# Kept slots leave the ring of weight buffers, and the output projection's last column block of the second token tile runs in two halves

## The chip, the core and the metric

The kernel runs on one core of a Trainium2 chip. Its time is the device time of one execution in microseconds (us), and the figure that counts is the median of several runs. The core has five engines that run side by side and wait for one another through semaphores. PE (TensorE) multiplies matrices. DVE (VectorE), ACT (ScalarE) and POOL (GpSimd) work element by element. SP (SyncE) issues nearly all of the DMA transfers, one after the other: a transfer that has to wait holds up every transfer behind it.

## What is computed

The input is 256 tokens of 2048 numbers, all float32. One block is computed: an RMS norm, an input projection, two kinds of attention heads, an output projection that is added to the input, and then a mixture of 32 experts in four groups. A router picks the best group and in it the best two experts for each token. What matters here is cut from the reference:

```python
x = x + mixed @ w_out[layer]
h = rms_norm(x, ffn_norm_gain[layer])
x = x + hierarchical_moe(h, w_group_router[layer], b_group_router[layer], ...)
...
g_prob = softmax(t @ w_group_router + b_group_router)        # 4 groups, top 1
e_all  = t @ w_expert_router + b_expert_router               # 32 experts, top 2 in the group
hid = jax.nn.silu(t @ wg) * (t @ wu)                         # for each of 32 experts
acc = acc + c[:, None] * (hid @ wd)
...
return rms_norm(x, final_norm_gain)
```

Every expert's three weight matrices (2048x512, 2048x512 and 512x2048, 4 MB each) are read from memory once, 384 MB in all.

## The kernel before, in words

The tokens lie in two tiles of 128, in `x2[:, t]`. The program has three stages: the input projection and the attention (up to about 280 us), the output projection with norm and router, and the experts (from about 415 us).

**Output projection, norm and router.** `w_out` is taken in four row quarters and in each in four column blocks of 512 (NB = 4). Only the last quarter matters here. `unit_parts` (L233) loads a piece of weights and splits it into a high and a low part (`wh`, `wl`), and `rows3` (L273, products in L277 to L279) multiplies high by high, low by high and high by low into one accumulator `acc` per token tile. After a column block, DVE adds the accumulator to `x2`. Between these products PE does the router's work on the blocks that are ready: `norm_T` (L578) squares the block on ACT for the norm's sum (`ss2`), transposes it on PE (L584) and copies it out on ACT (`hrT`, L586), and `logits` (L589, L593) multiplies it by the router's weights into `lg`. The last column block (L609 to L625) runs all its products for token tile 0, adds them (L622), runs all for tile 1, adds them, and then does `norm_T` and `logits` for both tiles. Nine products without use (L630) keep PE busy afterwards. DVE waits for `lg` and for the reciprocal root that POOL takes (`rst`, L156), and runs a chain of some twenty short operations (L646 to L732) up to the matrix `S0`, which gathers the tokens of the first two experts.

**Experts.** The loop at the end of the program takes two experts at a time, 16 pairs e = 0, 2, ..., 30. A pair runs its gate products (`pg`, 64 matmuls), its up products (`pu`, 64), gathers the next pair's tokens, and runs its down products (`y`, 64); a pair's results are added to `x2` while the next pair runs (`scatter`, L863; `yh` and `yl` are the weighted results, L859 and L860). Nearly all matmuls of this stage are issued by the helper `mm` (L761), in the order in which the program writes them (`keep_in_program_order`); the tile names tell them apart. The other engines' order, and SP's, comes from a scheduler.

**The ring.** The weights of a pair come in 12 loads of 2 MB, each into a slot of 16 KB per partition from `next_slot` (L748). The first 12 slots come from the list `first` (L744). After that the list `order`, which is `first` without `ring_h` and `ring_e`, is gone round: two slots from the pool `ring_r`, one from `ring_c`, four from `ring_a`, one from `ring_c`, two from `ring_d`. That is ten entries for ten buffers. A load into a buffer waits until PE has used what lay there.

Two of the slots are not for weights. In pair e = 28, `gates` takes one (L982) for the final gain and the output rows of token tile 0 (`gfin`, `fo[0]`). It is slot 172 of the count (14 pairs of 12, and 4 loads), which is the first entry of the list, `ring_r`, and it is kept to the program's end. In the last pair `down_cols` takes slot 193 for the output rows of token tile 1 (`fo[1]`, L1048). The list goes on as if both were ordinary: slots 182 and 183, the second and third gate load of the last pair, are `ring_r` again, slot 192 (the last down columns) is `ring_r`, and so is slot 193. With the kept slot in it, `ring_r` has one buffer left, which all four of these use.

**The end.** The last pair's down products run by columns (`down_cols`, L1023): four cuts of 512, 512, 512 and 384 columns and one of 128 (j = 0 to 4). `finish(j)` adds cut j to `x2` and calls `final_block` (L918): ACT squares the cut for the final norm and writes the squares into `fo[t]` (L921), then DVE (t = 0) or POOL (t = 1) overwrites that with the row times the gain (L924). `final_store` (L926) takes the reciprocal root, scales the rows and stores them.

Of the kernel before, what the change touches and what calls it, by code (L numbers as in the profile page):

```python
# [13 lines left out]
F32 = mybir.dt.float32  # L14
# [3 lines left out]
AF = mybir.ActivationFunctionType  # L18
OP = mybir.AluOpType
# [3 lines left out]
P = 128  # L23
T = 256
D = 2048
KC = D // P
NB = 4
# [53 lines left out]
def block_kernel(ctx: ExitStack, tc: tile.TileContext, a: dict, out: bass.AP):  # L81
    nc = tc.nc
    sync, act, dve, pe, pool = nc.sync, nc.scalar, nc.vector, nc.tensor, nc.gpsimd
    scale = 1.0 / math.sqrt(HD)

    con = ctx.enter_context(tc.tile_pool(name="con", bufs=1))
    ring_a = ctx.enter_context(tc.tile_pool(name="ring_a", bufs=NA))

    def slot(pl):
        return pl.tile([P, 4096], F32, tag="slot", name="slot")  # L90
# [27 lines left out]
    x2 = con.tile([P, 2, D], F32, name="x2")  # L118
# [154 lines left out]
    def rows3(accs, lh, ll, wh, wl, start, stop, tiles=(0, 1)):  # L273

        for t in tiles:
            tt = slice(t * P, (t + 1) * P)
            pe.matmul(accs[t], lh[:, tt], wh, start=start, stop=False)  # L277
            pe.matmul(accs[t], lh[:, tt], wl, start=False, stop=False)
            pe.matmul(accs[t], ll[:, tt], wh, start=False, stop=stop)  # L279
# [287 lines left out]
    sync.dma_start(wr, a["w_router"])  # L567
    sync.dma_start(c4, a["consts4"])
    dve.tensor_tensor(wr, wr, gfn[:, :, None].to_broadcast([P, KC, NG + NE]), op=OP.mult)
    ss2 = con.tile([P, 2, NB], F32, name="ss2")  # L570
    lg = rt_ps.tile([P, 2, NG + NE], F32, name="lg")

    def pt2():
# [1 line left out]

    hTs = {}

    def norm_T(b, t):  # L578

        sq = rt.tile([P, 512], BF, name="sq2")  # L580
        act.activation(sq, x2[:, t, b * 512:(b + 1) * 512], AF.Square, accum_out=ss2[:, t, b:b + 1])
        pt = pt2()
        for i in range(4):
            pe.transpose(pt[:, i * P:(i + 1) * P], x2[:, t, b * 512 + i * P:b * 512 + (i + 1) * P], ident)  # L584
        hT = rt.tile([P, 4, P], F32, name="hrT", bufs=2)
        act.activation(hT.rearrange("p a b -> p (a b)"), pt, AF.Copy)  # L586
        hTs[b, t] = hT

    def logits(b, t):  # L589
        for i in range(4):  # L590
            c = 4 * b + i

            pe.matmul(lg[:, t], hTs[b, t][:, i], wr[:, c], start=c == 0 and t == 0, stop=c == KC - 1 and t == 1,  # L593
                      skip_group_check=True)

    def tick0(b):
# [11 lines left out]

    accs = acc2()  # L609
    parts = list(unit_parts(a["w_out"], 3, (NB - 1) * 512))  # L610
    for t in range(2):
        for hf, wh, wl in parts:
            for j in range(2):
                c = 2 * hf + j
                rows3(accs, mh[3][:, c], ml[3][:, c], wh[:, j], wl[:, j], c == 0, c == 3, (t,))
            if t == 0:
                (tick0, tick1)[hf](NB - 1)
            elif hf == 0:
                logits(NB - 2, 0)
                logits(NB - 2, 1)  # L620
        xb = x2[:, t, (NB - 1) * 512:]
        dve.tensor_tensor(xb, xb, accs[t], op=OP.add)  # L622
    norm_T(NB - 1, 0)
    norm_T(NB - 1, 1)
    logits(NB - 1, 0)  # L625
    logits(NB - 1, 1)

    wps = pt2()
    for _ in range(NKEEP):
        pe.matmul(wps[:, :T], ident, hTs[NB - 1, 1][:, :2], start=True, stop=True)  # L630


    rst = con.tile([P, 2], F32, name="rst")
# [108 lines left out]
    y_ps = ctx.enter_context(tc.tile_pool(name="y_ps", bufs=4, space=PSUM, reuse_waits="tile"))  # L742

    first = [ring_r, ring_r, ring_c, ring_a, ring_h, ring_a, ring_e, ring_a, ring_a, ring_c, ring_d, ring_d]  # L744
    order = [q for q in first if q not in (ring_h, ring_e)]
    units = [0]

    def next_slot():  # L748
        units[0] += 1
        u = units[0] - 1  # L750
        return slot(first[u] if u < len(first) else order[(u - len(first)) % len(order)])

    def ps_m():
        return m_ps.tile([P, 512], F32, tag="m", name="m")
# [215 lines left out]
    def gates(e, gather_first):  # L970

        last = e == NE - 2
        pg = gu_ps.tile([P, F], F32, name="pg")
        pu = gu_ps.tile([P, F], F32, name="pu")
        for b in range(4):
            if gather_first is not None:
                hT[b] = gather(gather_first, b, 2 if e == 0 else 1)
            gate_up(pg, a["w_gate"], e, b)
        scatter_done((0, 1))
        cT = scatter_mat(sels_of(e))  # L980
        if e == NE - 4:
            z = next_slot()  # L982
            gfin[0], fo[0] = z[:, :D], z[:, D:]
            for b in range(NB):
                final_gain(b)
        for b in range(4):
            gate_up(pu, a["w_up"], e, b, last and b > 1)
            if last and b < 2:
                scatter_done((b + 2,))
        if e == 0:  # L990
            keep_rows()
        return cT, hidden(pg, pu, 2 if last else 1)
# [30 lines left out]
    def down_cols(e, cT, hid):  # L1023


        cuts = [(0, 512), (512, 1024), (1024, 1536), (1536, 1920), (1920, D)]
        w = {}
        for h in range(2):
            z = next_slot().rearrange("p (e c n) -> p e c n", e=2, c=2)
            for i in range(2):  # L1030
                sync.dma_start(z[:, i], a["w_down"][e + i, h * 256:h * 256 + 256, :1024]
                               .rearrange("(c p) n -> p c n", p=P))
                for j in range(2):
                    for c in range(2):
                        w[j, i, 2 * h + c] = z[:, i, c, j * 512:j * 512 + 512]
        for j in range(2, 5):
            n0, n1 = cuts[j]
            n = n1 - n0
            if n0 % 512 == 0:
                z = next_slot()  # L1040
                at0 = 0
            for i in range(2):
                zi = z[:, at0:at0 + 4 * n].rearrange("p (c n) -> p c n", c=4)
                at0 += 4 * n
                sync.dma_start(zi, a["w_down"][e + i, :, n0:n1].rearrange("(c p) n -> p c n", p=P))
                for c in range(4):
                    w[j, i, c] = zi[:, c]
        fo[1] = next_slot()[:, :D]  # L1048
        py = [ps_y() for _ in cuts[:4]]

        def products(j, cs):
            n = cuts[j][1] - cuts[j][0]
            for c in cs:
                for i in range(2):
                    mm(py[j][C * i:C * i + C, :n], hid[:, c, C * i:C * i + C], w[j, i, c],
                       start=c == 0, stop=c == 3)

        def finish(j):
            n0, n1 = cuts[j]

            scatter(cT, weighted(cT, py[j], n1 - n0), n0, n1,
                    lambda t: gu_ps.tile([P, F], F32, name="pu" if j % 2 else "pg") if t else ps_m())
            final_block(n0, n1, j)

        for h in range(2):
            for j in range(2):
                products(j, (2 * h, 2 * h + 1))
        for j in range(2, 5):
            if j == 4:
                py.append(ps_y())  # L1070
            finish(j - 2)
            products(j, range(4))
        finish(3)
        finish(4)
        final_store(len(cuts))
# [106 lines left out]
```

## Time and profile before

| | |
|---|---|
| median of 3 runs | 1364.29 us (1363.77 to 1365.88) |
| profiled execution, its own time | 1366.4 us |
| its span on the core | 1364.6 us |
| mean granted clock of PE | 0.988 of full speed |
| PE busy | 1308.2 us (96%) |
| ACT, DVE, POOL busy | 274.0, 491.8, 13.6 us |
| moved by DMA | 478.42 MB, mean 351 GB/s |

The profile is of one execution. Its page gives a string of digits for each engine: the span in 40 slices of 34.1 us, and in each the busy share in tenths. A busy PE is not a PE at its peak, since matmuls overlap and their ends are modelled. The views that answer questions about a place are the timeline (instructions by start time, what the engine waited for in brackets) and the stretches (busy time, clock and DMA rate between two times).

### The profile page before, as it was taken

Reading aid. Unit: us, or ns where it says so; the run is one execution under the profiler, and the core shown is the slowest. Engines: PE = TensorE matmul, PEld = TensorE weight load, DVE = VectorE, ACT = ScalarE, POOL = GpSimd, SP = SyncE. Lnnn points to the kernel's source line nnn. Section 1 sums busy time; section 2 is a strip of 40 time slices with the busy share of each in tenths; the row PEclk is TensorE's granted clock in tenths of the full one; section 3 lists DMA queues with packets and bytes.
Section 4 is the critical chain, followed back from the end, with each engine's and each line's share of the span. In section 5 each row is a group of like instructions: output and inputs, shape, how many; then the busy total and the mean of one; then the engine's idle time right before and its main releaser. Section 6 shows DMA issues by size and latency. Waiting matters only on the chain. (4 is left out here: it accounts for less than half of the span.)

```text
span 1364.6 us, 16713 instructions
## 1 busy us (share of the span) xinstructions
PE 1308.2 (96%) x7155; PEld 768.1 (56%) x7155; DVE 491.8 (36%) x906; ACT 274.0 (20%) x454; POOL 13.6 (1%) x22
## 2 busy tenths in 40 slices
PE   9999999999999999999999999999999999999885
PEld 8999998988885444535535444343543434343432
DVE  5555567677643121222322213212221322122123
ACT  6454445354340100000000000000000000001002
POOL 0000000000000000000000000000000000000001
PEclk9999999999999999999999999999999999998988
DMA  9973554446969799999999999999999999999793
GB/s 357 332 261 127 182 186 148 161 166 237 324 232 392 296 428 426 426 427 427 426 427 427 426 426 427 425 427 427 426 428 426 426 428 426 425 427 427 293 407 107
DMA packets 77223, 478.42 MB, mean 351 GB/s; under 512 B 5204, under 2 KB 8148, under 8 KB 53336
## 3 DMA queue, kind: packets, MB, share of 16 engines
q1 hardware_dynamic: 76848, 476.73, 86.0%
q8 instruction: 58, 0.95, 0.3%
q10 hardware_dynamic: 296, 0.56, 0.1%
q14 instruction: 21, 0.17, 0.0%
HBM read 475.18 MB, written 2.10 MB: 350 GB/s over the span
## 5 line engine op out<-in xcount | busy, mean ns | idle before, releaser
L761 PE MATMUL pu<-slot,hT 128*64 128x512 f32 x1024 | 235.2, 601 | 13.5 <-DMA slot<-in_w_up 13.5
L761 PE MATMUL pg<-slot,hT 128*64 128x512 f32 x1024 | 234.3, 598 | 12.3 <-DMA slot<-in_w_gate 12.3
L761 PE MATMUL y<-slot,hid 128*64 128x512 f32 (+2 forms) x1040 | 223.9, 587 | 0.1
L761 PEld LDWEIGHTS pg<-slot,hT 128*64 128x64 f32 x1024 | 75.3, 138 | 165.7 <-issue 153.5
L870 DVE TENSOR_TENSOR x<-x,y 128x512 f32<-128x512 f32 x120 | 75.9, 684 | 252.4 <-PE y L761 252.4
L761 PEld LDWEIGHTS pu<-slot,hT 128*64 128x64 f32 x1024 | 73.9, 138 | 163.7 <-issue 142.8
L761 PEld LDWEIGHTS y<-slot,hid 128*64 128x64 f32 x1040 | 72.8, 137 | 138.5 <-issue 136.0
L257 DVE TENSOR_TENSOR wl<-slot,wh 128x1024 fp32r<-128x1024 f32 (+1 forms) x100 | 117.6, 1181 | 81.5 <-ACT wh L256 81.0
L294 PE MATMUL acc<-xh,wh 128*128 128x256 f32 x512 | 131.5, 289 | 0.0
L294 PE MATMUL acc<-xl,wh 128*128 128x256 f32 x512 | 128.2, 283 | 0.0
L256 ACT ACTIVATE wh<-slot 128x1024 fp32r<-128x1024 f32 (+1 forms) x100 | 101.9, 1025 | 124.5 <-PE acc L279 72.6
L761 PE MATMUL m<-S,slot 128*128 128x128 f32 x960 | 113.7, 277 | 4.7 <-DVE hT L805 4.7
L761 PEld LDWEIGHTS m<-S,slot 128*128 128x128 f32 x960 | 110.5, 192 | 9.7 <-DVE hT L805 7.6
L860 DVE SCALAR_TENSOR_TENSOR yl<-y,ws,yh 128x512 fp32r<-128x512 f32 (+1 forms) x65 | 46.9, 741 | 166.7 <-ACT yh L859 165.1
L294 PEld LDWEIGHTS acc<-xl,wh 128*128 128x128 f32 x512 | 98.0, 191 | 0.4
L294 PEld LDWEIGHTS acc<-xh,wh 128*128 128x128 f32 x512 | 97.9, 191 | 0.5
L859 ACT ACTIVATE yh<-y,ws 128x512 fp32r<-128x512 f32 (+1 forms) x65 | 44.2, 680 | 254.9 <-PE y L761 254.9
L294 PE MATMUL acc<-xh,wl 128*128 128x256 f32 x512 | 82.3, 283 | 0.0
L838 DVE TENSOR_TENSOR sg<-sg,pu 128x512 f32<-128x512 f32 (+1 forms) x17 | 11.1, 655 | 192.6 <-PE pu L761 184.3
L805 DVE TENSOR_TENSOR hT<-m,smallp 128x512 f32<-128x512 f32 (+1 forms) x68 | 44.9, 660 | 91.7 <-PE m L761 91.7
L851 ACT ACTIVATE hid<-m 128x512 f32<-128x512 f32 (+1 forms) x17 | 9.7, 572 | 323.5 <-PE m L764 323.5
L294 PEld LDWEIGHTS acc<-xh,wl 128*128 128x128 f32 x512 | 70.6, 192 | 0.0
(215 smaller groups left out, 1131.8 us busy)
## 6 DMA issues: line engine op xcount, KB each, us to landing
slot<-in_w_down SPq DMA_DIRECT2D x60, 2048.0 KB, 32.6
slot<-in_w_gate SPq DMA_DIRECT2D x60, 2048.0 KB, 36.8
slot<-in_w_up SPq DMA_DIRECT2D x58, 2048.0 KB, 30.6
slot<-in_w_in SPq DMA_DIRECT2D x46, 1024.0 KB, 7.3
slot<-in_w_out SPq DMA_DIRECT2D x16, 1024.0 KB, 5.3
slot<-in_w_up SPq DMA_DIRECT2D x10, 1024.0 KB, 11.6
slot<-in_w_gate SPq DMA_DIRECT2D x8, 1024.0 KB, 9.6
slot<-in_w_down SPq DMA_DIRECT2D x6, 1024.0 KB, 16.1
```

Of the source, the lines that this page charges most:

```text
L256: act.activation(wh[:, k:k + n], src[:, k:k + n], AF.Copy)
L257: dve.tensor_sub(wl[:, k:k + n], src[:, k:k + n], wh[:, k:k + n].bitcast(F32))
L294: pe.matmul(o, wz[:, i * P:(i + 1) * P], x, start=k == 0 and i % 2 == 0 and wz is wh and x is h, stop=k == KC - 1 and i % 2 == 1 and wz is ...
L761: tc.keep_in_program_order(pe.matmul(*args, **flags))
L805: dve.tensor_tensor(hT[:, j * n:(j + 1) * n], p.rearrange("p (a b) -> p a b", a=n), (gfp if hp_ else gfn)[:, c:c + n, None].to_broadcast([ ...
L838: dve.tensor_tensor(sg[:, q], sg[:, q], pu[:, q], op=OP.mult)
L851: act.activation(hid[:, j * n:(j + 1) * n].rearrange("p c q -> p (c q)"), p[:, :n * P], AF.Copy)
L859: act.activation(yh[:, :n], py[:, :n], AF.Copy, scale=ws)
L860: dve.scalar_tensor_tensor(yl[:, :n], py[:, :n], ws, yh[:, :n].bitcast(F32), op0=OP.mult, op1=OP.subtract)
L870: dve.tensor_tensor(xb, xb, p[:, :n], op=OP.add)
```

## The change

`next_slot` now takes entries off the front of a queue and puts them back at its end, unless the slot is kept (or is `ring_h` or `ring_e`). The slots for `gfin` and `fo[0]`, and for `fo[1]`, are asked for with `keep=True`. After slot 172 the queue therefore holds nine entries: one `ring_r` and the eight others.

The output projection's last column block is written out anew. Token tile 0 runs as before. Token tile 1 runs in two halves of 256 columns: twelve products for a half, an addition of 256 columns to `x2`, then norm, transposes and the copy of that half. `norm_T` and `logits` take the range of 128-column pieces to work on, and `ss2` has a fifth column for the second half's sum, and is zeroed once by POOL.

```diff
-    ss2 = con.tile([P, 2, NB], F32, name="ss2")
+    ss2 = con.tile([P, 2, NB + 1], F32, name="ss2")
+    pool.memset(ss2, 0.0)
...
-    def norm_T(b, t):
+    def norm_T(b, t, i0=0, i1=4):
...
-    for t in range(2):
+    for hf, wh, wl in parts:
+        for j in range(2):
+            c = 2 * hf + j
+            rows3(accs, mh[3][:, c], ml[3][:, c], wh[:, j], wl[:, j], c == 0, c == 3, (0,))
+        (tick0, tick1)[hf](last)
+    xb = x2[:, 0, last * 512:]
+    dve.tensor_tensor(xb, xb, accs[0], op=OP.add)
+
+    for s in range(2):
+        n0 = s * 256
         for hf, wh, wl in parts:
             for j in range(2):
                 c = 2 * hf + j
...
+                o, h, l = accs[1][:, n0:n0 + 256], mh[3][:, c, P:], ml[3][:, c, P:]
+                for k, (x, w) in enumerate(((h, wh), (h, wl), (l, wh))):
+                    pe.matmul(o, x, w[:, j, n0:n0 + 256], start=s == 0 and c == 0 and k == 0,
+                              stop=s == 1 and c == 3 and k == 2, skip_group_check=True)
+            if hf == 0:
+                logits(last - 1, s)
+        xb = x2[:, 1, last * 512 + n0:last * 512 + n0 + 256]
+        dve.tensor_tensor(xb, xb, accs[1][:, n0:n0 + 256], op=OP.add)
+        if s == 0:
+            norm_T(last, 0)
+            norm_T(last, 1, 0, 2)
+        else:
+            logits(last, 0)
+            end = norm_T(last, 1, 2, 4)
+    logits(last, 1)
...
-    def next_slot():
-        units[0] += 1
-        u = units[0] - 1
-        return slot(first[u] if u < len(first) else order[(u - len(first)) % len(order)])
+    ring = deque(first)
+
+    def next_slot(keep=False):
+
+        q = ring.popleft()
+        if not keep and q not in (ring_h, ring_e):
+            ring.append(q)
+        return slot(q)
...
-            z = next_slot()
+            z = next_slot(keep=True)
...
-        fo[1] = next_slot()[:, :D]
+        fo[1] = next_slot(keep=True)[:, :D]
```

SP's queue, kernel before, at the loads of the last pair. A slot's number names the load, `DMAHW` is a transfer that must have landed and `PE_49` a matmul that must be done. `slot_7665` and `slot_7683` are the second and third gate load:

```order
L895 DMA slot_7665<-in_w_gate 128x4096 [waits DMAHW5_49,DMAHW4_49,PE_49]
L895 DMA slot_7685<-in_w_gate 128x4096 [waits PE_49]
L895 DMA slot_7735<-in_w_up 128x4096 [waits DMAHW6_49,PE_49]
L895 DMA slot_7683<-in_w_gate 128x4096 [waits DMAHW7_49,DMAHW4_49,PE_49]
L895 DMA slot_7737<-in_w_up 128x4096 [waits DMAHW0_49]
L887 DMA slot_7775<-in_w_up 128x2048 [waits DMAHW1_49]
```

The same place in the changed kernel, where the gate loads are `slot_7682` to `slot_7704`:

```order
L913 DMA slot_7684<-in_w_gate 128x4096 [waits DMAHW5_49,DMAHW4_49,PE_49]
L913 DMA slot_7702<-in_w_gate 128x4096 [waits PE_49]
L913 DMA slot_7704<-in_w_gate 128x4096 [waits DMAHW6_49,PE_49]
L913 DMA slot_7754<-in_w_up 128x4096 [waits DMAHW7_49,PE_49]
L913 DMA slot_7756<-in_w_up 128x4096 [waits DMAHW0_49,PE_49]
L905 DMA slot_7794<-in_w_up 128x2048 [waits DMAHW1_49,PE_49]
```

The third gate load stood behind the first up load and waited for the matmuls of the second gate load, whose buffer it takes; the loads behind it waited for no matmul. Now the four gate loads stand together, and each load behind them waits for the matmuls of the load that had its buffer nine entries earlier.

PE's queue at the end of the output projection, kernel before (L277 to L279 the products of token tile 1, L584 transposes, L593 router products, L630 the products without use):

```order
L277 MATMUL acc<-wh,mh 128x512
L278 MATMUL acc<-wl,mh 128x512
L279 MATMUL acc<-wh,ml 128x512
L584 MATMUL pt<-c_78,x_80 128x128 x8
L593 MATMUL lg<-wr,hrT 128x36 x8
L630 MATMUL pt<-hrT,c_78 128x256 x9
```

The same place in the changed kernel (L631 the products of half a block, L586 transposes, L597 router products):

```order
L631 MATMUL acc<-wh,mh 128x256
L631 MATMUL acc<-wl,mh 128x256
L631 MATMUL acc<-wh,ml 128x256
L597 MATMUL lg<-wr,hrT 128x36 x6
L586 MATMUL pt<-c_78,x_80 128x128 x2
L597 MATMUL lg<-wr,hrT 128x36 x2
L647 MATMUL pt<-hrT,c_78 128x256 x9
```

Of the last block's eight transposes, six have moved ahead of the second half's products, and two remain behind them, but after six router products.

ACT's queue in the last pair's end, kernel before (L921 the squares, in the order token tile 0, token tile 1 of a cut; L859 the weighting of a cut's products):

```order
L921 ACTIVATE slot,fss<-x_80 128x512 [waits DVE_49]
L859 ACTIVATE yh_4255<-y,ws 128x384 [waits PE_49,Activation_49]
L921 ACTIVATE slot,fss<-x_80 128x512 [waits DVE_49]
L921 ACTIVATE slot,fss<-x_80 128x512 [waits DMAHW4_49,DMAHW5_49,DMAHW2_49,DMAHW6_49,DMAHW0_49,DMAHW7_49,PE_49,Pool_49]
L921 ACTIVATE slot,fss<-x_80 128x512
L921 ACTIVATE slot,fss<-x_80 128x512 [waits DVE_49]
L921 ACTIVATE slot,fss<-x_80 128x384 [waits DVE_49] x2
L859 ACTIVATE yh_4253<-y,ws 128x128 [waits Activation_49]
L921 ACTIVATE slot,fss<-x_80 128x128 [waits DVE_49] x2
```

The same place in the changed kernel (L939 the squares, L877 the weighting):

```order
L939 ACTIVATE slot,fss<-x_80 128x512 [waits DVE_49] x2
L877 ACTIVATE yh_4274<-y,ws 128x384 [waits PE_49,Activation_49]
L939 ACTIVATE slot,fss<-x_80 128x512 [waits DVE_49] x2
L877 ACTIVATE yh_4272<-y,ws 128x128 [waits PE_49,Activation_49]
L939 ACTIVATE slot,fss<-x_80 128x384 [waits DVE_49] x2
L939 ACTIVATE slot,fss<-x_80 128x128 [waits DVE_49] x2
```

Before, the squares of token tile 1 waited for PE's last use of the down columns in the same buffer and stood together ahead of the last weighting. Now those of a cut stand in pairs, and the last weighting stands ahead of the fourth cut's.

## Rows read from the trace of the kernel before

**Rows 1.** The page: DMA rate in the 40 slices, and the gate products' group.
```profile
GB/s 357 332 261 127 182 186 148 161 166 237 324 232 392 296 428 426 426 427 427 426 427 427 426 426 427 425 427 427 426 428 426 426 428 426 425 427 427 293 407 107
...
L761 PE MATMUL pg<-slot,hT 128*64 128x512 f32 x1024 | 234.3, 598 | 12.3 <-DMA slot<-in_w_gate 12.3
```

**Rows 2.** Timeline of PE: start, duration (us), line, tile, count, wait before it.
```profile
473.63 13.90 PE L761 MATMUL pg<-slot,hT 128*64 128x512 f32 x64
...
1270.48 13.95 PE L761 MATMUL y<-slot,hid 128*64 128x512 f32 x64
1284.27 7.04 PE L761 MATMUL pg<-slot,hT 128*64 128x512 f32 x32
1299.18 9.45 PE L761 MATMUL pg<-slot,hT 128*64 128x512 f32 x32 [7.88 <-DMA slot<-in_w_gate]
```

**Rows 3.** Timeline of SP's DMA issues, 1255 to 1295 us.
```profile
1260.32 0.33 SPq L895 DMA_DIRECT2D slot<-in_w_up  x1
1291.34 0.33 SPq L895 DMA_DIRECT2D slot<-in_w_gate  x1
```

**Rows 4.** Stretches: length, busy time per engine, clock, DMA share, GB/s.
```profile
460.00:465.00 5.00, 5.00 (x24) 1.62 (x24) 1.53 (x5) 0.00 (x0) 0.00 (x0) 1.00 0.29 59
...
1280.00:1290.00 10.00, 10.00 (x50) 3.43 (x48) 1.50 (x2) 1.37 (x2) 0.00 (x0) 1.00 0.26 111
1290.00:1300.00 10.00, 2.12 (x10) 0.47 (x6) 0.00 (x0) 0.00 (x0) 0.00 (x0) 0.69 0.78 297
```

**Rows 5.** Timeline of all engines, the last pair's end.
```profile
1346.21 1.09 PE L761 MATMUL y<-slot,hid 128*64 128x128 f32 x16
...
1347.40 0.64 ACT L921 ACTIVATE slot<-x 128x512 f32<-128x512 f32 x1
...
1348.20 3.73 POOL L924 TENSOR_TENSOR slot<-x,slot 128x512 f32<-128x512 f32 x3 [939.48 <-ACT slot L921]
...
1348.67 0.55 DVE L870 TENSOR_TENSOR x<-x,pu 128x384 f32<-128x384 f32 x1
...
1350.27 0.35 ACT L859 ACTIVATE yh<-y,ws 128x128 fp32r<-128x128 f32 x1
1350.65 0.35 DVE L860 SCALAR_TENSOR_TENSOR yl<-y,ws,yh 128x128 fp32r<-128x128 f32 x1 [1.43 <-ACT yh L859]
1350.66 0.33 PE L761 MATMUL m<-yh,cT 128*128 128x128 f32 x1 [2.15 <-ACT yh L859]
```

**Rows 6.** Timeline of all engines, the end of the output projection and the router.
```profile
404.19 0.48 PE L277 MATMUL acc<-wh,mh 128*128 128x512 f32 x1
404.50 0.39 PE L278 MATMUL acc<-wl,mh 128*128 128x512 f32 x1
...
405.65 0.60 PE L584 MATMUL pt<-c,x 128*128 128x128 f32 x4
...
405.85 0.69 DVE L622 TENSOR_TENSOR x<-x,acc 128x512 f32<-128x512 f32 x1 [4.73 <-PE acc L279]
...
407.08 2.08 PE L593 MATMUL lg<-wr,hrT 128*128 128x36 f32 x16
...
407.45 0.59 ACT L586 ACTIVATE hrT<-pt 128x512 f32<-128x512 f32 x1
...
408.02 0.70 POOL L156 TENSOR_TENSOR rst<-rst,half_c 128x2 f32<-128x2 f32 x1 [82.73 <-DVE rst L155]
...
409.27 0.42 DVE L646 SCALAR_TENSOR_TENSOR L<-lg,rst,rbias 128x36 f32<-128x36 f32 x2 [1.33 <-PE lg L593]
```

**Rows 7.** Stretches of products of 512 columns (330 to 350 us) and of 256.
```profile
330.00:350.00 20.00, 20.00 (x90) 16.57 (x89) 13.50 (x16) 8.22 (x8) 0.00 (x0) 1.00 0.82 286
250.00:270.00 20.00, 20.00 (x169) 20.00 (x168) 12.58 (x22) 8.08 (x14) 0.00 (x0) 1.00 0.59 208
```

**Rows 8.** Timeline: operations of 256 columns out of PSUM, on DVE and on ACT.
```profile
416.13 0.43 DVE L805 TENSOR_TENSOR hT<-m,smallp 128x256 f32<-128x256 f32 x1 [0.97 <-PE m L761]
...
1329.07 0.78 ACT L851 ACTIVATE hid<-m 128x256 f32<-128x256 f32 x2 [17.17 <-PE m L764]
```

More of the change, by code (lines that the diff above doesn't have):

```diff
@@ L576, in block_kernel, with logits @@
     hTs = {}
-    def norm_T(b, t):
+    def norm_T(b, t, i0=0, i1=4):
+        c0, n = b * 512 + i0 * P, (i1 - i0) * P
         sq = rt.tile([P, 512], BF, name="sq2")
-        act.activation(sq, x2[:, t, b * 512:(b + 1) * 512], AF.Square, accum_out=ss2[:, t, b:b + 1])
+        act.activation(sq[:, :n], x2[:, t, c0:c0 + n], AF.Square, accum_out=ss2[:, t, b + (i0 > 0):b + (i0 > 0) + 1])
         pt = pt2()
-        for i in range(4):
-            pe.transpose(pt[:, i * P:(i + 1) * P], x2[:, t, b * 512 + i * P:b * 512 + (i + 1) * P], ident)
+        for i in range(i1 - i0):
+            pe.transpose(pt[:, i * P:(i + 1) * P], x2[:, t, c0 + i * P:c0 + (i + 1) * P], ident)
         hT = rt.tile([P, 4, P], F32, name="hrT", bufs=2)
[L586 to L590, printed above, removed]
+        act.activation(hT[:, :i1 - i0].rearrange("p a b -> p (a b)"), pt[:, :n], AF.Copy)
+        for i in range(i0, i1):
+            hTs[b, t, i] = hT[:, i - i0]
+        return hT
+    def logits(b, t, i0=0, i1=4):
+        for i in range(i0, i1):
             c = 4 * b + i
-            pe.matmul(lg[:, t], hTs[b, t][:, i], wr[:, c], start=c == 0 and t == 0, stop=c == KC - 1 and t == 1,
+            pe.matmul(lg[:, t], hTs[b, t, i], wr[:, c], start=c == 0 and t == 0, stop=c == KC - 1 and t == 1,
                       skip_group_check=True)
@@ L610, in block_kernel @@
     parts = list(unit_parts(a["w_out"], 3, (NB - 1) * 512))
-    for t in range(2):
+    last = NB - 1
+    for hf, wh, wl in parts:
[7 more added lines that the diff above has]
+        n0 = s * 256
         for hf, wh, wl in parts:
@@ L614, in block_kernel @@
                 c = 2 * hf + j
[L615 to L626, printed above, removed]
+                o, h, l = accs[1][:, n0:n0 + 256], mh[3][:, c, P:], ml[3][:, c, P:]
[13 more added lines that the diff above has]
+    logits(last, 1)
     wps = pt2()
     for _ in range(NKEEP):
-        pe.matmul(wps[:, :T], ident, hTs[NB - 1, 1][:, :2], start=True, stop=True)
+        pe.matmul(wps[:, :T], ident, end[:, :2], start=True, stop=True)
     rst = con.tile([P, 2], F32, name="rst")
@@ L744, in block_kernel @@
     first = [ring_r, ring_r, ring_c, ring_a, ring_h, ring_a, ring_e, ring_a, ring_a, ring_c, ring_d, ring_d]
-    order = [q for q in first if q not in (ring_h, ring_e)]
-    units = [0]
-    def next_slot():
-        units[0] += 1
-        u = units[0] - 1
-        return slot(first[u] if u < len(first) else order[(u - len(first)) % len(order)])
+    ring = deque(first)
[4 more added lines that the diff above has]
+        return slot(q)
     def ps_m():
```

## The prediction

> **What bounds the kernel now.** I read the page's slices first. From the 15th slice (about 478 us) to the 37th the DMA rate is 425 to 428 GB/s: the expert stage is bound by its loads. The 38th (1262 to 1296 us) drops to 293, and none before it in that stage does [rows 1]. What PE lacks there the page's groups tell: over the whole run it idled 12.3 us ahead of gate products, for their weights [rows 1].
>
> PE's timeline shows 7.88 of these 12.3 us in one wait. The down products of pair 28 run to 1284.3, the first 32 gate products of the last pair follow, and the next 32 start only at 1299.18; they also take 9.45 us where the 32 before took 7.04 [rows 2]. In the stretches DMA carries 111 GB/s from 1280 to 1290, and from 1290 to 1300 the granted clock is 0.69 on average, so part of that stretch ran at 1.2 GHz instead of 2.4 [rows 4]. SP shows why: it issues an up load at 1260.32 and nothing more until 1291.34 [rows 3], when the gate products of the load that lies in the wanted buffer are done.
>
> Last I read the end. The last cut's products start at 1346.21 and take 1.09 us, but PE's next work on them starts at 1350.66, after 2.15 us of waiting for ACT [rows 5]. From 1347.40 ACT ran the squares that could not start until PE was done with the buffer of `fo[1]`, and it came to the last weighting at 1350.27 [rows 5].
>
> **Part one: the loads.** Behind the changed `next_slot`, slot 183 is `ring_c`, and the fourth gate load takes the `ring_a` buffer, and the place in SP's queue, that an up load had. That was issued at 1260.32 [rows 3], and so will this be. From there I count who frees what. The next up load takes a buffer free at about the same time. The two after it take buffers of pair 28's down products, half of which are done at 1270.48 + 13.95/2 = 1277.5; two more come free at 1284.3, two at 1291.3 and the last at 1298.2 [rows 2]. In before, the transfers in flight moved 111 GB/s x 10 us = 1.1 MB after 1280 [rows 4], some 2.6 us of work at 427 GB/s. One load of 2 MB more (4.9 us) keeps DMA busy to 1287.5, and by then the loads freed at 1277.5 and 1284.3 are queued. So DMA does not run dry.
>
> PE then runs its 64 gate products in one go, as in a pair without such a wait, in 13.90 us [rows 2]: to 1284.27 + 13.90 = 1298.17, instead of 1299.18 + 9.45 = 1308.63. That is **10.46 us**, 7.88 of it the wait, nearly all the rest the low clock. What would be late next? Eight loads remain behind the gate at 4.9 us each. The first two land at 1287.5 and 1292.4, and the up products that need them cannot start before 1298.2; the last lands near 1322, and the last cut's products start at 1346.21 - 10.46 = 1335.75. PE is the bound from there on, and it hides the loads with 6 us or more in hand. If that cover went, PE would wait again, by up to the same 10.46. I keep 8.5 to 10.6 as bounds.
>
> **Part two: the end.** `fo[1]` now lies in a `ring_a` buffer whose gate weights were used up some 40 us earlier, so ACT squares token tile 1 of a cut right behind tile 0. In before's times: from 1347.40 on one square stands there instead of five, the last weighting comes at 1347.40 + 0.64 = 1348.04 instead of 1350.27, and DVE is later than ACT: its addition of the fourth cut ends at 1348.67 + 0.55 = 1349.22, and the last low part (`yl`) stands behind it on DVE. That starts at about 1349.15 instead of 1350.65 [rows 5]. So the gain is **1.5 us**, not 2.2. Bounds: nothing, should ACT or POOL stand in the way in another form, and 2.2.
>
> **Part three: the router.** I follow PE's own queue, since PE is the last to finish there: DVE waited 1.33 us for `lg` until 409.27, while POOL had `rst` at 408.02 + 0.70 = 408.72 [rows 6].
>
> Products of 256 columns come every 20/169 = 0.118 us, of 512 every 20/90 = 0.222 [rows 7]; 24 for 12 cost 24 x 0.118 - 12 x 0.222 = +0.17. The Trainium skill, page "TensorE: Matmul & The Clock Gate", section "Back-to-back issue gap", gives N/2.4 + 2.5 ns instead; by it the exchange would cost 0.03 us, and the forecast would be 0.14 lower. The trace does not agree with so small a price, and I keep the rows'.
>
> The first product behind other work is followed after 404.50 - 404.19 = 0.31 us, 0.085 more than usual [rows 6, 7]; two more such changes cost +0.17. Six transposes move ahead of the products' end, at 0.10 each (four take 0.60, some 0.2 of it drain [rows 6]): +0.60. So the products' end moves from 405.65 [rows 6] to 406.6.
>
> Behind it stand six router products at 0.21 each (eight take 2.08, some 0.37 of it drain [rows 6]), to 407.85, and only then the two last transposes. The half addition takes 0.43 [rows 8] instead of 0.69 [rows 6] and is done at 407.2, so the transposes wait for PE's queue, not for it. They end at 408.2, ACT's copy takes 0.39 [rows 8] to 408.6, and the last two products with their drain 0.80: 409.4. Before, four products and the drain stood behind a copy that ended at 407.45 + 0.59 = 408.04 [rows 6]. POOL's root, behind the half addition and half a square, comes at about 408.9. So DVE starts at 409.4 instead of 409.27, **0.15 us later**: what is saved behind the last product is paid ahead of it. Were POOL the last, it would be 0.4 earlier than before; were the first half's addition to hold PE for its whole length, 0.5 later than I have it. I take +0.15, since each term has its row, and the bounds -0.4 to +0.7.
>
> This passes to the end one for one, because DMA is not yet the bound: from 460 to 465 us it carries only 59 GB/s [rows 4], waiting for buffers that PE frees. The one memset on POOL waits for nothing and stands at the program's start, hidden by the attention stage.
>
> **Sum.** 10.46 + 1.5 - 0.15 = 11.8. The profiled execution would go from a span of 1364.6 to 1352.8, and from 1366.4 to 1354.6. It lies 2.1 above the median of the runs shown, 1364.29, so I take the 11.8 off the median: **1352.5 us**. With the bounds (8.5 + 0 - 0.7 = 7.8 and 10.6 + 2.2 + 0.4 = 13.2) it is 1351.1 to 1356.5. Single runs lie up to 1.6 us off the median. A measurement of this kernel tells a change of 0.2%, 2.7 us, from none.
>
> **Rivals.** *The wait moves on.* SP issues in order, and behind the fourth gate load stand one up load and then one that waits for half of pair 28's down products. If DMA has nothing left when they are done, the up products wait where the gate products did. For it: the same queue held everything back for 31 us before [rows 3]. Against it: they are half done at 1277.5, ten us before the queued loads end. Price: up to the whole 10.46, so 1352.5 + 10.5 = 1363, or something between. Chance 0.05.
>
> *The end gives nothing back.* POOL's three multiplications (3.73 us, 1.24 each [rows 5]) ran late and alone before. Now each may meet DVE's multiplication of the same cut. If the third holds DVE up for its length, 1.24 of the 1.5 go, and the time is 1353.7. For it: both start when a cut's squares are done. Against it: DVE's comes one square, 0.64 us, earlier. Chance 0.10. The Trainium skill, page "SBUF — State Buffer", section "Who interferes with whom", says that a DVE instruction with two SBUF inputs and a GpSimd instruction that reads SBUF share a port, and that the later one is blocked. This is such a pair; no row here shows one running beside the other.
>
> *Slower: the clock falls in the router.* Small products and waits for copies now stand between the projection's last halves and the first experts. If PE's clock falls to 1.2 GHz there and stays, the first pair's gate and up products, 13.9 us each at 2.4 GHz, take twice as long and the loads wait with them: 1352.5 + 28 = 1380. It decides from 11.8 us lost, that is with nearly all the gate products slow. For it: the clock was down after 7.88 us of waiting [rows 2, 4]. Against it: PE's wait for the last copy, 408.2 to 408.6, is a twentieth of that. Chance 0.02.
>
> *The change does not do what it says*, the pools handing out the same buffers: only the router's 0.15 is left, 1364.4. SP's queue speaks against it, in which each late load now has a matmul of its own to wait for. Chance 0.01.
>
> **How the numbers follow.** The forecast, 1352.5, has 0.82, with its own range of 1350.8 to 1354.6 from the runs' spread and the terms' bounds. Taking in the second rival and the mild part of the first, the range that should hold 8 in 10 is 1350.8 to 1355.2. Faster by more than 0.2% are the forecast, the second rival and some half of the first: 0.82 + 0.10 + 0.03 = 0.95. Within 0.2% are the rest of the first and the last rival: 0.03. Slower: 0.02.
>
> **What would show it.** Loads: SP issues the last pair's four gate loads without a gap of more than 10 us before the fourth, the 38th slice's DMA rate stays above 400 GB/s, and the 64 gate products stand in one row of about 13.9 us at a clock of 1.0. End: the squares of a cut stand in pairs, and PE waits under 0.5 us for the last `yh`. Router: DVE starts `L` within 0.5 us of 409.4 with PE as its releaser. The forecast is wrong if PE waits more than 1 us for a DMA after 1284, or if the first experts start more than 1 us away from before's time.

## The result, and the profile after

The changed kernel takes **1344.59 us** (median of 4 runs, 1343.64 to 1347.39), the kernel before 1364.03 beside it: a ratio of 0.9861, 95% interval 0.9849 to 0.9874, or 17 to 21 us gained. The forecast was 1352.5, with a range down to 1350.8. So it named the right side and stopped short by 7.9 us.

Three pieces of the profile answer to rows of before. First the loads. The page's DMA slices and its group of gate products:

```profile
GB/s 364 335 262 132 189 164 151 177 138 259 310 235 378 275 429 431 431 429 431 430 430 430 432 428 431 431 430 431 430 431 429 431 432 429 430 431 430 431 419 147
...
L779 PE MATMUL pg<-slot,hT 128*64 128x512 f32 x1024 | 230.8, 593 | 1.4 <-DMA slot<-in_w_gate 1.2
```

The hole in the 38th slice is gone (431 in place of 293, [rows 1]), and PE waits 1.2 us for gate weights over the whole run, not 12.3. But every slice from the 15th on reads higher too: 428 to 432 where before had 425 to 428. Nothing in the forecast asked for that. SP's queue, and PE's timeline from pair 28's down products on:

```profile
1227.23 23.35 SPq L913 DMA_DIRECT2D slot<-in_w_gate  x4
1250.67 17.18 SPq L913 DMA_DIRECT2D slot<-in_w_up  x2
1267.95 10.75 SPq L905 DMA_DIRECT2D slot<-in_w_up  x6
```

```profile
1260.42 13.95 PE L779 MATMUL y<-slot,hid 128*64 128x512 f32 x64
1274.20 13.90 PE L779 MATMUL pg<-slot,hT 128*64 128x512 f32 x64
```

SP issues the four gate loads as one group and does not stand still for 31 us behind them [rows 3]. The 64 gate products are one row of 13.90 us with no wait, where [rows 2] had two rows and 7.88 us between them.

The last cut, all engines, with the two multiplications (DVE's and POOL's) of the cut before:

```profile
1323.35 0.68 DVE L942 TENSOR_TENSOR slot<-x,slot 128x512 f32<-128x512 f32 x1
...
1323.61 1.55 POOL L942 TENSOR_TENSOR slot<-x,slot 128x512 f32<-128x512 f32 x1 [3.18 <-ACT slot L939]
...
1325.69 1.09 PE L779 MATMUL y<-slot,hid 128*64 128x128 f32 x16
...
1326.05 0.63 ACT L939 ACTIVATE slot<-x 128x512 f32<-128x512 f32 x1 [0.72 <-DVE x L888]
...
1327.06 0.68 DVE L942 TENSOR_TENSOR slot<-x,slot 128x512 f32<-128x512 f32 x1
...
1327.29 0.35 ACT L877 ACTIVATE yh<-y,ws 128x128 fp32r<-128x128 f32 x1
1327.46 1.41 POOL L942 TENSOR_TENSOR slot<-x,slot 128x512 f32<-128x512 f32 x1 [2.30 <-ACT slot L939]
...
1327.83 0.22 PE L779 MATMUL m<-yh,cT 128*128 128x128 f32 x1
...
1328.62 0.34 DVE L878 SCALAR_TENSOR_TENSOR yl<-y,ws,yh 128x128 fp32r<-128x128 f32 x1
...
1329.01 0.33 PE L779 MATMUL m<-yl,cT 128*128 128x128 f32 x1 [0.96 <-DVE yl L878]
...
1332.12 3.33 SPq L957 DMA_DIRECT2D out_dram<-slot  x4
```

The weighting `yh` comes 1.60 us after the products' start instead of 4.06 [rows 5], and PE's wait is now the one for `yl`, as the forecast had it. The first store is issued 1332.12 - 1325.69 = 6.43 us after the products' start. In before it was 7.95:

```profile
1354.16 4.49 SPq L939 DMA_DIRECT2D out_dram<-slot  x4
```

To see where the time came from I cut both profiled executions at the same marks of the program. PE's rows at the marks that [rows 2, 5] do not have, of before and then of after:

```profile
414.72 2.27 PE L761 MATMUL m<-S,x 128*128 128x128 f32 x16 [1.26 <-DVE S L732]
...
733.57 13.95 PE L761 MATMUL y<-slot,hid 128*64 128x512 f32 x64
...
1205.13 13.95 PE L761 MATMUL y<-slot,hid 128*64 128x512 f32 x64
```

```profile
413.99 2.27 PE L779 MATMUL m<-S,x 128*128 128x128 f32 x16 [1.26 <-DVE S L749]
...
732.87 13.95 PE L779 MATMUL y<-slot,hid 128*64 128x512 f32 x64
...
1198.35 13.95 PE L779 MATMUL y<-slot,hid 128*64 128x512 f32 x64
```

| stretch | before, us | after, us | gained |
|---|---|---|---|
| start to the first gather product | 414.72 | 413.99 | 0.73 |
| to the down products at 733 | 318.85 | 318.88 | -0.03 |
| to those at 1205 (1198) | 471.56 | 465.48 | **6.08** |
| pair 28, to its down products | 65.35 | 62.07 | **3.28** |
| to the last cut's products | 75.73 | 65.27 | 10.46 |
| to the end of the span | 18.39 | 16.21 | 2.18 |
| sum | 1364.6 | 1341.9 | 22.7 |

The two stretches that the forecast was about gave 10.46 and 2.18 (10.46 and 1.5 were forecast). Another 9.4 us come from two stretches in which it saw nothing change. (Between these two executions 22.7 us; between the medians 19.4, since before's profiled run lies 2.4 us above its median and after's 1.0 below.)

Much of the 3.28 in pair 28 has a reason of its own. There the eight products of the final gain, `m<-g`, stand ahead of the up products. The last six of them and the up products, before and after, and the granted clock (the last number but two) first in before and then in after:

```profile
1238.56 4.89 PE L761 MATMUL m<-g,c 4*128 4x512 f32 x6 [0.33 <-DVE cT L790]
1243.38 16.92 PE L761 MATMUL pu<-slot,hT 128*64 128x512 f32 x64
```

```profile
1231.55 2.90 PE L779 MATMUL m<-g,c 4*128 4x512 f32 x6 [0.32 <-DVE cT L808]
1234.70 15.53 PE L779 MATMUL pu<-slot,hT 128*64 128x512 f32 x64 [0.25 <-DMA slot<-in_w_up]
```

```profile
1239.00:1242.00 3.00, 3.00 (x5) 1.21 (x4) 1.62 (x4) 0.82 (x2) 0.00 (x0) 0.52 1.02 431
1242.00:1245.00 3.00, 3.00 (x6) 0.53 (x6) 0.00 (x0) 0.97 (x2) 0.00 (x0) 0.50 0.99 421
```

```profile
1235.00:1238.00 3.00, 3.00 (x8) 0.70 (x6) 0.00 (x0) 0.08 (x1) 0.00 (x0) 0.52 0.99 415
```

The clock falls to 1.2 GHz (0.5 of full speed) here in both kernels, earlier and for longer in this execution of before. The profiles of the experiments below show that this differs from one execution to the next.

### The profile page after: what moved, and what is told of

Same layout as the page of the kernel before. It is cut to its first block, busy times and chain, and to the rows that moved or that the text cites. A ratio compares the mean times of both kernels' runs of the same rounds, so it can differ in the third digit from the quotient of the medians.

```text
span 1341.9 us, 16745 instructions
## 1 busy us (share of the span) xinstructions
PE 1299.4 (97%) x7167; PEld 768.4 (57%) x7167; DVE 491.8 (37%) x907; ACT 274.7 (20%) x457; POOL 14.4 (1%) x23
## 4 chain that ended last, share of the span: by engine, by line
PE 76%; DMA 20%; DVE 3%; issue 0%; ACT 0%; SPq 0%; POOLq 0%; DVEq 0%; POOL 0%
DMA slot<-in_w_up 20%; PE y L779 16%; PE acc L294 14%; PE pu L779 13%; PE m L779 9%; PE pg L779 8%; PE acc L277 4%; PE acc L278 4%; PE acc L279 4%; DVE hT L823 1%; DVE x L888 1%; PE lg L597 1%; PE ps L190 0%; PE ps L411 0%; PE ps L340 0%
## 5 line engine op out<-in xcount | busy, mean ns | idle before, releaser
L779 PE MATMUL pg<-slot,hT 128*64 128x512 f32 x1024 | 230.8, 593 | 1.4 <-DMA slot<-in_w_gate 1.2
L877 ACT ACTIVATE yh<-y,ws 128x512 fp32r<-128x512 f32 (+1 forms) x65 | 44.2, 680 | 253.6 <-PE y L779 253.6
```

The costliest lines, as they stand in the source:

```text
L779: tc.keep_in_program_order(pe.matmul(*args, **flags))
L877: act.activation(yh[:, :n], py[:, :n], AF.Copy, scale=ws)
```

## The experiments

My theory for the 6 us was an **address**. `ss2` grew from 32 to 40 bytes per partition, for which the pool gives 64, so everything behind it starts 32 bytes later. By the allocator's addresses, which no trace shows, the eight buffers of `ring_a`, `ring_c` and `ring_d` start at byte 20992 and so on, a multiple of 512, where before had 20960, which is 480 past one. (`ring_r`, `ring_h` and `ring_e` are counted from the other end and did not move.) PE's own pace did not change: from the first gather product to the down products at 733 us it takes 318.8 to 318.9 us in all eleven profiles of whole kernels. The rivals: the rate belongs to the run, or to the order of the ring.

**The shift alone, in the kernel before.**
```diff
     ss2 = con.tile([P, 2, NB], F32, name="ss2")
+    pool.memset(con.tile([P, 8], F32, name="pad"), 0.0)
```


> Before, with one 32-byte tile added to the constants, so that the eight ring buffers of ring_a, ring_c and ring_d start 32 bytes later in each partition, as they do in the changed kernel (a multiple of 512 in place of 32 bytes less than one). Nothing else changes. Address theory: the loads run faster because of where the buffers start. The steady slices then show 430 to 431 GB/s in place of 426 to 427, and the time is 1364.0 - 6.1 = 1357.9 us (6.1 us is what the changed kernel gained between the down products of the pairs at 733 and 1205 us). Rival, the rate belongs to the run or to the ring's order: 1364.0 us and 427 GB/s.

Measured: 1355.68 us against 1364.01, ratio 0.9931 [0.9917, 0.9945], so 7.5 to 11.3 us gained by a tile that no one reads (8.3 by the medians, 2.2 more than expected). Its slices:

```profile
GB/s 366 325 263 127 185 184 139 175 151 236 321 236 397 285 430 431 430 431 430 430 431 431 427 432 431 430 430 430 431 432 429 430 430 430 430 431 430 288 416 96
```

The steady slices read 427 to 432, nearly all of them 430 or 431, with the hole in the 38th (288) still there. The rate follows the shift, with the ring as it was.

**The ring's change alone.**
```diff
-    order = [q for q in first if q not in (ring_h, ring_e)]
-    units = [0]
+    ring = deque(first)
...
-            z = next_slot()
+            z = next_slot(keep=True)
```


> Before with the ring's change alone: kept slots take their entry out, the constants keep their size and the ring buffers their old addresses, and the router stays as it was. Address theory: only the last pair's stretch is shorter, by the 12.6 us that the two profiles differ by from pair 28's down products on, so 1364.0 - 12.6 = 1351.4 us, with 427 GB/s in the steady slices. Rival, the order of the ring brings the rate: 1345.3 us with 430 GB/s.

Measured: 1353.71 us, ratio 0.9911 [0.9897, 0.9924], 10.4 to 14.0 us gained (10.3 by the medians, 2.3 less than expected). The steady slices stay at before's rate and the hole is filled:

```profile
GB/s 358 330 267 130 187 174 140 186 135 249 314 246 379 286 428 424 426 426 427 428 427 427 427 426 427 427 427 426 426 427 427 427 427 426 426 426 427 427 407 121
```

Pair 28's down products and the last cut's products:

```profile
1270.94 13.95 PE L762 MATMUL y<-slot,hid 128*64 128x512 f32 x64
...
1336.20 1.09 PE L762 MATMUL y<-slot,hid 128*64 128x128 f32 x16
```

From the one to the other it takes 65.26 us against 75.73, and from there 16.5 to the end of its span of 1352.7, against 18.39. Both terms are the ring's, and the rate is not.

**The shift taken back, in the changed kernel** (one more 32-byte tile, so that the eight start 32 bytes past a multiple of 512).
```diff
     ss2 = con.tile([P, 2, NB + 1], F32, name="ss2")
+    pool.memset(con.tile([P, 8], F32, name="pad"), 0.0)
```


> The changed kernel with one more 32-byte tile among the constants, so that the eight ring buffers start 32 bytes past a multiple of 512. Address theory: the rate falls back to about 427 GB/s and the time rises by some 6 us to 1350.7. Rival: 1344.6 us as the changed kernel, with 430 GB/s.

Measured: 1352.99 us, ratio 0.991 [0.9897, 0.9924], 2.3 us more than expected; the steady slices are back at 425 to 429:

```profile
GB/s 356 340 265 126 186 180 138 183 139 246 315 246 382 284 428 426 426 426 427 427 426 429 428 426 427 426 427 426 427 427 425 426 427 427 427 427 427 427 409 138
```

That is the whole change without the favourable address, and it lands 0.5 us from the forecast.

**Ring and shift without the halves.** The second and the first of these edits in one kernel; the output projection and the router are those of before.

> The ring's change and the 32-byte tile, but no halves in the output projection, norm and router. Address theory: the changed kernel plus the 0.7 us by which its router stage ends earlier, 1344.6 + 0.7 = 1345.3 us; the first gather product starts at 414.7 and not 414.0 us. Rival, the halves have a larger part in the gain than their stage shows: 1351 us.

Measured: 1344.64 us, ratio 0.985 [0.9837, 0.9864], the same as the changed kernel. The halves give nothing that shows. The part on the first gather product was wrong: it starts at 413.66, not at 414.7. But eight transposes that stand on PE ahead of all that the change touches start 28.05 us before it there (385.61); in before the two are 28.07 apart (386.65), in after 27.99 (386.00). So 0.65 of the 0.73 us in the table's first line was there ahead of the changed code, and the halves gave 0.08.

**The address by itself: nothing but loads.**
```diff
+    def load(off):
+        z = ring.tile([P, 4224], F32, tag="slot", name="slot")[:, off:off + 4096]
...
+        sync.dma_start(z.rearrange("p (k f) -> p k f", k=8), ...)
```


> Nothing but loads: the block's computation is left out and zeros are stored. 224 expert loads of 2 MB go through eight buffers, in seven stages of 32 loads whose buffers start 0, 480, 32, 64, 128, 256 and again 0 bytes past a multiple of 512 in each partition. Address theory: the rate depends on where a load is written, whoever reads it. The stages with 480 and 32 then move about 0.9% less than those with 0 (427 against 430.5 GB/s), the last stage equals the first, and the stages with 64, 128 and 256 tell how fine the grid is. Rival, the rate fell in the kernel before because the engines read their operands from addresses that are off by 32 bytes: all seven stages are equal within 0.2%.

Stretches well inside the seven stages, in order; the last number is GB/s:

```profile
20.00:140.00 120.00, 0.00 (x0) 1.00 1.01 431
180.00:300.00 120.00, 0.00 (x0) 1.00 1.01 428
340.00:460.00 120.00, 0.00 (x0) 1.00 1.01 428
500.00:610.00 110.00, 0.00 (x0) 1.00 1.01 428
650.00:770.00 120.00, 0.00 (x0) 1.00 1.01 428
810.00:920.00 110.00, 0.00 (x0) 1.00 1.01 431
960.00:1060.00 100.00, 0.00 (x0) 1.00 1.01 431
```

0, 256 and again 0 bytes past a multiple of 512 run at 431; 480, 32, 64 and 128 past run at 428. No engine reads these buffers, so it is the load itself that is slower. What is read does not decide: by the kernel's text the stages with 0 and 128 read the same experts, so do those with 480 and 256, and those with 32 and 0 again, and in each of these couples the rate differs. (It is one execution, with 32 loads a stage.) More exactly from SP's queue, where an issue marks the landing eight loads earlier: 28 loads from the third of the stage with 0, and 28 from the third of the stage with 480:

```profile
18.19 0.33 SPq L97 DMA_DIRECT2D slot<-in_w_gate  x1
...
154.32 0.33 SPq L97 DMA_DIRECT2D slot<-in_w_gate  x1
...
173.90 0.33 SPq L97 DMA_DIRECT2D slot<-in_w_gate  x1
...
311.19 0.33 SPq L97 DMA_DIRECT2D slot<-in_w_gate  x1
```

136.13 / 28 = 4.862 us a load against 137.29 / 28 = 4.903, 0.85% more. The same count gives 4.914 for 32, 4.895 for 64, 4.894 for 128 and 4.860 for 256. The Trainium skill, page "DMA: Bandwidth & Descriptors", section "How a descriptor splits into AXI transactions", says that a descriptor is cut into transactions of 256 bytes which have to start at multiples of 256, and that one which starts elsewhere begins with a transaction from the boundary below. These runs agree with the grid of 256, for the address that is written; the page speaks of what is read, and no run here moved that.

**64 bytes past, in the whole kernel.**
```diff
+    pool.memset(con.tile([P, 16], F32, name="pad"), 0.0)
```


> The changed kernel with a 64-byte tile among the constants, so that the eight ring buffers start 64 bytes past a multiple of 512. If a multiple of 64 is all that counts: 1344.6 us and 430.5 GB/s. If the grid is 256 or 512 bytes: 1353 us and 427 GB/s, as with 32 bytes past.

Measured: 1350.65 us, ratio 0.9902 [0.9888, 0.9916], with 425 to 429 GB/s in the steady slices. A multiple of 64 does not do. The loss of 6 us against the changed kernel is smaller than the 8.4 with 32 bytes past, in the same order as 4.895 and 4.914 us a load, but the two times are not apart beyond their intervals; the bytes moved, below, are.

**The last two buffers too.**
```diff
+    edge = ctx.enter_context(tc.tile_pool(name="edge", bufs=1, reuse_waits="tile", side="right"))
+    pool.memset(edge.tile([P, 56], F32, name="edge"), 0.0)
     ring_h = ctx.enter_context(tc.tile_pool(name="ring_h", bufs=1, ...
```


> The changed kernel with a 224-byte tile at the upper end of the partitions, so that the buffers of ring_r, ring_h and ring_e, which stood 480 bytes past a multiple of 512, start at multiples of 256 too. Address theory: two of the ten buffers in the steady rotation still had the slow address; the eight gave 8.4 us, two more give at most a quarter of it, 2.1 us: 1342.5 us, and 431 GB/s or a little more in the steady slices. Rival, only the eight mattered, or PE is the bound by now: 1344.6 us.

Measured: 1346.09 us, ratio 0.9872 [0.9857, 0.9886]: no gain over the changed kernel. Nor did the loads become faster by anything like a quarter of what the eight gave. What the queue of the loads moved from 500 to 1150 us (packets, MB, share of the 16 DMA engines), a line each of before, of the kernel with 64 bytes past, of after, and of this one:

```profile
q1 hardware_dynamic: 19003, 276.85, 100.4%
q1 hardware_dynamic: 19033, 277.27, 100.4%
q1 hardware_dynamic: 19168, 279.26, 100.5%
q1 hardware_dynamic: 19173, 279.31, 100.5%
```

The four profiles with the eight at 480 or 32 bytes past lie at 276.82 to 276.85 MB, and the five with the eight alone at multiples of 256 at 279.21 to 279.26. The eight give 0.87%, about as much as all eight give with nothing else running (0.85%), and the other two add at most 0.04%, where a quarter of 0.87% was to be expected. So my 2.1 us was wrong. Why these two buffers do not count stays open.

**The buffer of `fo[1]` alone, in the kernel before.**
```diff
-        fo[1] = next_slot()[:, :D]
+        fo[1] = slot(ring_a)[:, :D]
```


> Before, with the buffer of fo[1] taken from ring_a, where an up load of the last pair was used up, and nothing else changed. The end's term by itself: forecast 1.5 us, and by the five profiles so far 1.97 us (the last cut's products start 18.5 us before the end with the old buffer, 16.5 with the new one), so 1364.0 - 2.0 = 1362.0 us. Rival, the end gains only because the loads come earlier: 1364.0 us.

Measured: 1362.40 us (12 runs), ratio 0.9987 [0.9978, 0.9996], so 0.5 to 3.0 us gained. The last cut's products:

```profile
1342.48 1.09 PE L761 MATMUL y<-slot,hid 128*64 128x128 f32 x16
```

From there to the end it takes 1358.9 - 1342.48 = 16.4 us against 18.39. The end's term stands by itself.

**The gain products spread out**, an attempt at the low clock of pair 28.
```diff
-            for b in range(NB):
-                final_gain(b)
         for b in range(4):
+            if e == NE - 4:
+                final_gain(b)
             gate_up(pu, a["w_up"], e, b, last and b > 1)
```


> The changed kernel with the eight products of the final gain, which read four rows and stood together ahead of pair 28's up products, put two at a time ahead of each quarter of those up products. In nine profiles the clock fell to 1.2 GHz during or right after them: the last six and the 64 up products took 18.3 to 21.8 us together, against 2.9 + 13.9 = 16.8 without a low clock. Theory: this stretch alone makes most of the runs' spread, and without the low clock the time is 1344.6 - 3 = 1341.6 us, of a smaller spread (bounds: 1.5 to 5.0 us gained). Rival, the loads hold the pair up as soon as PE is faster there: 1344.6 us.

> The changed kernel once more, beside the one with the spread gain products: 1344.6 us, with more spread than the other; the last six gain products and the 64 up products of pair 28 again take between 18.3 and 21.8 us together.

Measured: 1348.09 us (ratio 0.9875 [0.9859, 0.9892]) against 1344.49 for the changed kernel beside it (0.9852 [0.9836, 0.9868]). Slower, by 3.6 us in the medians. The profile shows where, and the granted clock (0.79) of two microseconds inside PE's wait:

```profile
1229.81 1.12 PE L779 MATMUL m<-g,c 4*128 4x512 f32 x2
1234.42 6.40 PE L779 MATMUL pu<-slot,hT 128*64 128x512 f32 x16 [3.49 <-DMA slot<-in_w_up]
1240.75 1.12 PE L779 MATMUL m<-g,c 4*128 4x512 f32 x2
1241.80 3.65 PE L779 MATMUL pu<-slot,hT 128*64 128x512 f32 x16
```

```profile
1232.00:1234.00 2.00, 0.00 (x0) 0.00 (x0) 1.33 (x3) 0.00 (x0) 0.00 (x0) 0.79 1.02 426
```

Together, the gain products had filled time in which PE waits for up weights anyway. Spread out they leave a wait of 3.49 us, the clock falls during it (the first 16 up products take 6.40 us, the next 3.65), and six gain products must be run later, 1.05 us a pair. My theory was wrong, and so was the rival: the time rose. In the repeat of the changed kernel the six gain products and the up products take 3.03 + 15.37 = 18.4 us; over the ten profiles of whole kernels that have them in one place the sum lies between 18.3 and 21.8, after 18.4 and before 21.8, with no clear order by address (21.8 in the kernel with the shift alone at 430 GB/s, 18.3 in the one with the buffer of `fo[1]` alone at 427). So the table's 3.28 us is no more than this stretch differs by between kernels that hardly differ here, and most of it cannot be put down to the change.

## Why the prediction was right, and where it failed

- **The loads.** Right in mechanism and size: no wait, one row of gate products, SP's queue, DMA not dry. 10.46 us forecast, 10.46 measured in the table, and 75.73 - 65.26 = 10.47 in the kernel with the ring's change alone. The rival that the wait moves on is out: PE waits for no load after 1260.42 in after.
- **The end.** Right: 1.5 forecast, 7.95 - 6.43 = 1.52 measured up to the first store, and `yl` starts 1328.62 - 1325.69 = 2.93 us after the products (2.94 forecast). The other 0.66 of the table's 2.18 lie behind that issue, in the stores, which the change does not touch: 10.44 us to the end of the span in before, 9.78 in after. Over nine profiles with the new buffer the time from the last cut's products to the end is 16.2 to 16.9 us, against 18.39 and 18.59 with the old one. The second rival, that POOL holds DVE up, is out: POOL was the one that became slower. Its multiplications started 0.26 and 0.40 us after DVE's of the same cut, ran beside them for 0.42 and 0.28 us, and took 0.31 and 0.17 longer than the 1.24 of before.
- **The router.** Nothing instead of 0.15 lost; after's own stage is 0.08 shorter. PE was the releaser of `L`, as said. The sign that I gave for it was missed: DVE starts `L` at 408.55, 0.85 us before 409.4. But an absolute mark was of no use here: the eight transposes named above, which stand ahead of the changed code, start anywhere from 385.61 to 386.65 over the eleven profiles. Counted from them `L` comes 0.07 us earlier than in before (22.55 us against 22.62), where 0.15 later was forecast.
- **The step that failed** is this sentence: "The one memset on POOL waits for nothing and stands at the program's start, hidden by the attention stage." I costed the edit of `ss2` as an instruction and not as bytes. The tile's 32 bytes more moved eight ring buffers onto multiples of 256, and the loads became some 0.9% faster in a stage that I had called bound by its loads in my first paragraph. By the runs that is worth 8.3 us in the kernel before (1364.01 to 1355.68) and 8.4 in the changed one (1352.99 to 1344.59). Without it the forecast of 1352.5 is met by 1352.99 (single runs 1350.23 to 1353.61). No rival of mine covered a change of the rate itself.

How so little a load comes to some 8 us: 276.85 and 279.26 MB in 650 us are 4.924 and 4.881 us for 2 MB, 0.043 less. From the first steady slice at 478 us to pair 28's up products at 1243 that is some 155 loads, or 6.7 us. It shows only late, because the loads had a lead: up to 733 us both kernels run at PE's pace, 54.75 us a pair, and the loads' 12 x 4.924 = 59.1 or 58.6 sets it from there on. The stretch up to the pair at 1205, from which the runs' forecasts took their 6.1 us, leaves out what follows. The remaining 1.6 us lie within the intervals, and no run shows their place. Pair 28, up to its down products, averages 62.9 us in five profiles with the favourable address and 64.5 in five without, but single ones lie between 61.7 and 65.7.

## What to carry to other kernels

Where the loads bound a stage, look at the address of every buffer that they fill whenever a tile in front of it changes its size, and put the buffers on multiples of 256 bytes and measure what it gives; a pad of 32 bytes gave 8 us here, and moving two more buffers gave nothing. A part that looks free by its instructions can still move data. And before a total is explained, cut both executions at the program's own marks: here each forecast term was right to 0.7 us while the total was off by eight.

## What the runs showed of the hardware that I had not expected

- With nothing else running, a load of 2 MB takes 4.86 us into buffers that start 0 or 256 bytes past a multiple of 512, and 4.89 to 4.91 into ones 32, 64, 128 or 480 past. In the whole kernels eight buffers of ten showed the whole of this difference, and the other two none.
- POOL's multiplications of a cut took 1.55 and 1.41 us beside DVE's and 1.24 each when they ran late in before [rows 5]; DVE's own took 0.68 in both kernels. That DVE's work is the cause fits the overlaps but was not tried.
- Eight products of four rows in one place go with a fall of the granted clock to 1.2 GHz in all ten profiles of pair 28, and the last six of them with the up products take 18.3 to 21.8 us from profile to profile. Put two at a time, the four couples ran at a granted clock of 1.00, and the fall came in a wait of 3.49 us. What lowers the clock was not tried apart.
